# A hybrid decoder layer: S5 halves as two chains, recurrence gates two strips behind their input, ten gate strips ahead of the GLU, states through DRAM

## The chip, the core and the metric

The kernel runs on one core of a Trainium2 chip, in one launch. Its time is device microseconds (us) from launch to end, as the median of several executions; one more execution is taken with the hardware profiler, and all rows below come from that one. The core has a matmul engine (TensorE, PE in the rows; PEld are its weight loads), a vector engine (VectorE, DVE), an engine for activation functions (ScalarE, ACT), a general one (GpSimd, POOL), and SyncE (SP), whose queue issues every transfer between DRAM and on-chip memory (DMA).

## The reference

One decoder layer on 1024 tokens of width 1024, in fp32:

```
h  = rms_norm(x) ;  z = h @ w_in + b_in          # columns: u_a 512, u_b 1024, gate_a 1024, gate_b 1024
# S5 branch: 32 groups of 16 channels, 64 complex states each
s_t = A * s_{t-1} + B u_a ;  y = Re(C s) + d * u_a
z_a = gelu(y) ;  y_a = z_a * sigmoid(z_a @ w_glu + b_glu)
# RG-LRU branch
xc = causal conv of width 4 over u_b
r, i = sigmoid(xc @ w_r + b_r), sigmoid(xc @ w_i + b_i)      # 16 heads of 64
a = exp(-8 r softplus(-lambda)) ;  h_t = a h_{t-1} + sqrt(1 - a^2) i xc
merged = sigmoid(gate_a) * (y_a @ w_a_out) + sigmoid(gate_b) * (h @ w_b_out)
x = x + merged @ w_o
x = x + (silu(h2 @ w_gate) * (h2 @ w_up)) @ w_down           # h2 = rms_norm(x), hidden 2816
x = x + sigmoid(rms_norm(x) @ w_pg + b) * rms_norm(p @ w_ple)
out = rms_norm(x)
```

The change touches the S5 branch, the RG-LRU branch and the order of the matmuls between them; the feed-forward part and the end stay as they are.

## The kernel before, in words

Everything is held transposed: 128 channels on the partitions, 1024 tokens along the free axis; such a tile is a slot, and there are 43 slots (`NSLOT`, one pool, `slot`). A matmul in fp32 is done as three matmuls of a faster type: each operand is split into a high part (ACT copies it) and a low part (DVE subtracts), in `split` (L231, L232) for activations and in `prep_to` (L187, L188) for weights, and `mm3` (L220) adds high x high, high x low and low x high in PSUM. PSUM has four tiles of 128 x 1024; the same four serve the strips' sums (`mm`) and everything else (`sm`).

The work is a list of units (`add`, `plan`). A unit is one strip of 128 output channels: two chunks of four weight blocks, 48 matmuls in all (a GLU strip is one chunk of 24). `emit` traces a unit chunk by chunk: matmuls, then, behind the first chunk, the eviction of the unit before (`flush`), then the weights of later chunks, then one step (`tick`) of each running chain. A chain is a generator that does a piece of side work at each step; `drain` runs a chain to its end at once. Transfers, engine order and waits are then set by a planner that takes instructions in the traced order as they become ready; `tc.high_priority()` lets some go first. Engines work strictly in the order that the planner gives them.

Order of the units before: 8 units of `p @ w_ple`; 4 of u_a (`ev_ua` writes each to DRAM as `ud`); 9 gate strips (`add_gate`; gate_a 0 to 7 and gate_b 0, `ev_ga` and `ev_gb` scale them, take the sigmoid and write them to DRAM); 4 GLU strips; 1 gate strip; 8 of `w_a_out` (`add_ao`); then the 8 strips of u_b (`add_ub`, conv in `ev_ub` L576 and L579) with the small gate units of the recurrence (`add_ri`: 24 matmuls, r and i of 128 channels) one strip behind, and gate strips after strips 1, 2, 4 and 5, before the last gate unit and at the end; then 8 of `w_b_out`, 8 of `w_o`, and the rest.

S5 (`s5_all`) is one chain. `s5_params` prepares constants on POOL. `s5_setup(hf)`, six steps for each half of the groups: products of powers and B, C on DVE (L1319 to L1336), transposes (L1347), a convolution kernel for blocks of eight tokens (L1362 to L1369), which 16 transfers spread into `km`. `s5_data(hf)`: 16 transfers bring the half's input blocks from `ud` (`U`, L1413), `s5_tables` makes sine and cosine tables (ten DVE instructions, L1388 to L1398, and ACT's Abs and Sin), 64 matmuls project the input (L1432), twelve DVE instructions rotate it (L1440 to L1446), two scans and six more run the recurrence over blocks (L1448 to L1455), 96 matmuls make the output (`km` L1468, `wr`, `wi` L1473), and two copies (`Y`, L1480) and 32 transfers in all put it into `yd`. Both setups run one after the other, then the two halves' data steps take turns, one half at each step.

`pre_glu` drains S5 and then `load_z`, which for each of four tiles loads y from `yd`, takes gelu (`z`, L657) and splits it (`zh`, `zl`). The GLU's matmuls read these.

In the recurrence, `lru(m0)` takes strips in pairs, started by the eviction of the pair's second gate unit: exp, tanh, square (ACT, L610 to L616), products (DVE, L619, L621), sqrt (ACT, L623), product (L626), scan (DVE, L630). The eight states `yb` stay in slots until `yb_split` splits them for `w_b_out`; `pre_b` drains both.

Of the kernel before, what the change touches and what calls it, by code (L numbers as in the profile page):

```python
# [14 lines left out]
AF = mybir.ActivationFunctionType  # L15
ALU = mybir.AluOpType

P = 128
L = 1024
# [11 lines left out]
LOAD_AHEAD = 6  # L31
PREP_AHEAD = 4
DOWN_PARTS = (8, 7, 7)
GATES_FIRST = 9
UB_GATES = (1, 2, 4, 5)
X_POOL = ()
HEAD_UNITS = 10
TAIL_CUT = 768
# [56 lines left out]
class Build:  # L95
# [339 lines left out]
    def plan(self):  # L435
        nc, h = self.nc, self.h
# [5 lines left out]
        self.xd = self.dram([8, P, L], "xd")  # L442
        self.vd = self.dram([22, P, L], "vd")
        self.ud = self.dram([512, 8, P], "ud")
        self.yd = self.dram([512, 8, P], "yd")
        pt = {}

# [54 lines left out]
        for n2 in range(4):  # L502
            e = self.elem(lambda n2=n2: wple[n2 // 2][:, 512 * (n2 % 2):512 * (n2 % 2) + 512])
            for q in range(2):
                n = 2 * n2 + q
# [20 lines left out]
        def w_in(n):  # L526
            return self.chunks(h["w_in"][n], lambda k: xg[k])
# [33 lines left out]
        def add_gate():  # L561
            f, n, ev = gates.pop(0)
            self.add(f(n), ev)

        for m in range(GATES_FIRST):
            add_gate()


        xcs, xct, ri, yb = {}, {}, {}, {}

        def ev_ub(m):
            def ev(ps):
                u = scaled(ps, "x", "u")
                nc.scalar.activation(out=u, in_=u, func=AF.Identity, bias=self.v("b_in", 4 + m))
                xc = self.slot(name="xc")
                nc.vector.tensor_scalar(out=xc, in0=u, scalar1=self.v("conv_w", 24 + m), scalar2=self.v("conv_b", m),  # L576
                                        op0=ALU.mult, op1=ALU.add)
                for s in (1, 2, 3):
                    nc.vector.scalar_tensor_tensor(  # L579
                        out=xc[:, s:], in0=u[:, :L - s], scalar=self.v("conv_w", 8 * (3 - s) + m), in1=xc[:, s:],  # L580
                        op0=ALU.mult, op1=ALU.add)
                xct[m] = xc
                xcs[m] = self.split(xc, "xc")
            return ev

        def ri_mm(m):
            def mm(u, hi, lo, pairs):
                u.ps = [self.ps_sm(), self.ps_sm()]
                for q in range(2):
                    w = slice((2 * (m % 2) + q) * P, (2 * (m % 2) + q + 1) * P)  # L590
                    self.mm3(u.ps[q], hi[:, w], lo[:, w], xcs[m], True, True)
                xcs.pop(m)
            return mm

        def ev_ri(m):
            def ev(ps):
                for q, b in ((0, "b_r"), (1, "b_i")):
                    t = self.slot(name="ri")
                    nc.scalar.activation(out=t, in_=ps[q], func=AF.Sigmoid, bias=self.v(b, m))  # L599
                    ri[m, q] = t  # L600
                if m % 2 == 1:
                    self.lru_last = self.start(lru(m - 1))
            return ev

        def lru(m0):
            a, a2, th = {}, {}, {}
            ms = (m0, m0 + 1)
            for m in ms:
                a[m] = self.slot(name="a")
                nc.scalar.activation(out=a[m], in_=ri[m, 0], func=AF.Exp, scale=self.m8sp[:, m:m + 1])  # L610
            for m in ms:
                th[m] = ri.pop((m, 0))
                nc.scalar.activation(out=th[m], in_=th[m], func=AF.Tanh, scale=self.p8sp[:, m:m + 1])
            for m in ms:
                a2[m] = self.slot(name="a2")
                nc.scalar.activation(out=a2[m], in_=a[m], func=AF.Square)  # L616
            yield
            for m in ms:
                nc.vector.scalar_tensor_tensor(out=th[m], in0=a2.pop(m), scalar=1.0, in1=th[m],  # L619
                                               op0=ALU.add, op1=ALU.mult)  # L620
                nc.vector.tensor_tensor(out=ri[m, 1], in0=ri[m, 1], in1=xct.pop(m), op=ALU.mult)  # L621
            for m in ms:
                nc.scalar.activation(out=th[m], in_=th[m], func=AF.Sqrt)  # L623
            yield
            for m in ms:
                nc.vector.tensor_tensor(out=ri[m, 1], in0=ri[m, 1], in1=th.pop(m), op=ALU.mult)  # L626
            yield
            for m in ms:
                y = self.slot(name="yb")
                nc.vector.tensor_tensor_scan(out=y, data0=a.pop(m), data1=ri.pop((m, 1)), initial=0.0,  # L630
                                             op0=ALU.mult, op1=ALU.add)
                yb[m] = y
            yield

        ri_elem = {}
# [1 line left out]
        def add_ub(m):  # L637
            pre = None
            if m == 0:
                def pre():  # L640
                    self.lrup = self.start(self.lru_params())
            self.add(w_in(4 + m), ev_ub(m), pre=pre)

        def add_ri(m):
            if m // 2 not in ri_elem:
                ri_elem[m // 2] = self.elem(h["w_ri"][m // 2])
            self.add([(ri_elem[m // 2], None)], ev_ri(m), mm=ri_mm(m))


        ya, gl, mg, ybs = {}, {}, {}, {}  # L650

        def load_z():
            for m in range(4):
                y = self.slot(shape=(P, 8, P), name="y")
                nc.sync.dma_start(y, self.yd[m * P:(m + 1) * P])
                z = self.slot(name="z")
                nc.scalar.activation(out=z.rearrange("p (c j) -> p j c", j=8), in_=y, func=AF.Gelu_apprx_tanh)  # L657
                self.zs[m] = self.split(z, "z")
                self.zf[m] = z
                yield  # L660

        def load_g(kind, m):
            if m < 8 and (kind, m) not in gl:
# [1 line left out]
                nc.sync.dma_start(t, {"a": self.gad, "b": self.gbd, "p": self.apd}[kind][m])  # L665

        def pre_glu():
            self.drain(self.s5gen)
            self.drain(self.start(load_z()))

        def ev_glu(m):
            def ev(ps):
# [16 lines left out]
            return ev  # L689

        def yb_split():
            for m in range(8):
                while m not in yb:
                    yield
                ybs[m] = self.split(yb.pop(m), "yb")
                yield

        def pre_ao():
            load_g("a", 0)
# [4 lines left out]
        for m in range(4):  # L704
            add_glu(m)
            if m == 0:
                self.units[-1].pre = pre_glu
        add_gate()
        for m in range(8):
            add_ao(m)  # L710
        for m in range(8):
            add_ub(m)
            if m >= 1:
                add_ri(m - 1)
            if m in UB_GATES:
                add_gate()
        add_gate()
        add_ri(7)
        while gates:
            add_gate()  # L720
        self.units[-2].pre = lambda: setattr(self, "ybg", self.start(yb_split()))

        def pre_b():
# [393 lines left out]
    def s5_all(self):  # L1117
        self.zs, self.zf = {}, {}
        self.s5gen = self.chains[-1]
        yield from self.s5_params()  # L1120
        data = []
        for hf in range(2):
            yield from self.s5_setup(hf)
        while self.ua_done < 2:
            yield
        d0 = self.s5_data(0)
        d1 = self.s5_data(1)
        live = [d0]
        n = 0
        while live or n < 2:  # L1130
            if n < 2 and self.ua_done >= 4:
                n += 1
                if n == 2:
                    live.append(d1)
            for g in list(live):
                try:
                    next(g)
                except StopIteration:
                    live.remove(g)
                yield  # L1140

    def s5_params(self):
        nc, h = self.nc, self.h
# [261 lines left out]
    def s5_data(self, hf):  # L1405
        nc, st = self.nc, self.st

        us = []
        for i in range(2):
            u = self.slot(shape=(P, 8, P), name="U")  # L1410
            m = 2 * hf + i
# [25 lines left out]
        for q in range(2):  # L1437
            c = slice(512 * q, 512 * q + 512)
# [14 lines left out]
        nc.vector.tensor_tensor(out=co, in0=t2, in1=co, op=ALU.mult)  # L1453
        nc.vector.tensor_tensor(out=qr, in0=qr, in1=si, op=ALU.subtract)
        nc.vector.tensor_tensor(out=qi, in0=qi, in1=co, op=ALU.add)  # L1455
        yield
        wr, wi = st.pop(("w", hf))
        km = st.pop(("k", hf))
        psy = []
# [17 lines left out]
        for q in range(2):  # L1477
            m = 2 * hf + q
            y = self.slot(shape=(P, 8, P), name="Y")
            nc.scalar.activation(out=y.rearrange("p (a b) c -> p b a c", b=2),  # L1480
                                 in_=psy[q].rearrange("p (b a c) -> p b a c", b=2, a=4), func=AF.Copy)
# [70 lines left out]
```

## Time and profile before

| | us |
|---|---|
| median of 3 runs | 1487.66 (1486.79 to 1490.31) |
| profiled execution: time | 1488.67 |
| profiled execution: span, first to last instruction | 1486.7 |
| PE busy | 1423.7 (96% of the span) |
| DVE / ACT / POOL busy | 847.3 / 564.3 / 151.3 |
| TensorE's granted clock, mean | 0.976 of full speed |

PE's busy time counts matmuls at whatever clock is granted, so a stretch can be fully busy and still slow; the clock stands in a column of its own. In the rows, `out<-in` names tiles by their names in the program, with buffer numbers left out; a line number is that of the kernel, and can be that of a helper. Behind `<-` in square brackets stands what ended the idle time of the engine.

### The profile page before, as it was taken

The numbers are of one execution on the slowest core, as the hardware profiler recorded it, in microseconds if no ns is written. First come the engines' busy times: TensorE is split into PE (matmuls) and PEld (weight loads), VectorE is DVE, ScalarE is ACT, GpSimd is POOL, SyncE is SP. The second block draws the span as 40 slices with busy tenths as digits, with TensorE's granted clock in tenths as the row PEclk, the third lists the DMA queues.
The fourth block names the chain that finished last, engine by engine and source line by source line (L and its number), as shares of the span: only waits on it lengthen the run. The fifth ranks groups of instructions, "written<-read, shape, count | busy, mean of one in ns | idle before, by whom it ended". The sixth has DMA issues, their size and how long they took to land.

```text
span 1486.7 us, 16789 instructions
## 1 busy us (share of the span) xinstructions
PE 1423.7 (96%) x6586; PEld 1175.3 (79%) x6586; DVE 847.3 (57%) x988; ACT 564.3 (38%) x720; POOL 151.3 (10%) x250
## 2 busy tenths in 40 slices
PE   8899967999989899999999999999999999999995
PEld 6688856788878688887788888888888888888885
DVE  7366493535577774367566655555556224256486
ACT  7232132612554852144433333333335342123333
POOL 7910300000000000000000000000000021012243
PEclk9999987999999999999999999999999999999997
DMA  8322424351212144353122222222227442232222
GB/s 322 102 99 88 130 64 109 129 208 58 76 44 78 50 175 155 117 171 113 57 85 85 86 85 85 83 80 80 85 71 242 146 152 84 71 106 88 76 92 113
DMA packets 70318, 161.39 MB, mean 109 GB/s; under 512 B 11520, under 2 KB 23200, under 8 KB 70240
## 3 DMA queue, kind: packets, MB, share of 16 engines
q1 hardware_dynamic: 70240, 160.33, 32.0%
q8 instruction: 51, 0.84, 0.2%
q14 instruction: 27, 0.22, 0.0%
HBM read 118.23 MB, written 40.89 MB: 107 GB/s over the span
## 4 chain that ended last, share of the span: by engine, by line
PE 78%; DVE 7%; issue 5%; ACT 4%; POOL 4%; DMA 1%; SPq 1%; DVEq 0%; ACTq 0%; POOLq 0%
PE mm L220 47%; PE mm L312 28%; PE sm L220 1%; POOL x L963 1%; SPq L1483 1%; PE sm L392 0%; DVE x L1026 0%; DVE xc L579 0%; ACT ri L599 0%; DVE el L1016 0%; PE sm L1473 0%; ACT sq L410 0%; PE sm L377 0%; DMA s5p<-s5p 0%; DVE yb L630 0%
## 5 line engine op out<-in xcount | busy, mean ns | idle before, releaser
L187 ACT ACTIVATE whi<-raw 128x512 fp32r<-128x512 f32 (+1 forms) x158 | 97.3, 618 | 375.4 <-PE mm L220 322.9
L312 PE MATMUL mm<-twh,whi 128*128 128x512 f32 x528 | 206.5, 391 | 1.3 <-ACT pc L290 1.0
L312 PE MATMUL mm<-twl,whi 128*128 128x512 f32 x528 | 206.0, 390 | 0.8 <-DVE twl L232 0.8
L312 PE MATMUL mm<-twh,wlo 128*128 128x512 f32 x528 | 202.7, 390 | 0.0
L188 DVE TENSOR_TENSOR wlo<-raw,whi 128x512 fp32r<-128x512 f32 (+1 forms) x158 | 109.6, 696 | 128.8 <-ACT whi L187 128.8
L220 PE MATMUL mm<-xgh,whi 128*128 128x512 f32 x448 | 139.7, 393 | 0.0
L220 PE MATMUL mm<-xgh,wlo 128*128 128x512 f32 x448 | 138.0, 390 | 1.0 <-DVE wlo L188 1.0
L220 PE MATMUL mm<-xgl,whi 128*128 128x512 f32 x448 | 138.6, 390 | 0.0
L312 PEld LDWEIGHTS mm<-twh,whi 128*128 128x128 f32 x528 | 99.5, 188 | 23.1 <-ACT pc L290 1.4
L312 PEld LDWEIGHTS mm<-twl,whi 128*128 128x128 f32 x528 | 99.5, 189 | 22.0 <-DVE twl L232 1.1
L312 PEld LDWEIGHTS mm<-twh,wlo 128*128 128x128 f32 x528 | 99.4, 188 | 20.8
L174 ACT ACTIVATE whi<-wr 128x512 fp32r<-128x512 f32 x110 | 69.5, 632 | 105.7 <-PE mm L312 102.2
L220 PE MATMUL mm<-vh,wlo 128*128 128x512 f32 x352 | 109.0, 390 | 0.0
L220 PE MATMUL mm<-vl,whi 128*128 128x512 f32 x352 | 108.4, 389 | 0.0
L220 PE MATMUL mm<-vh,whi 128*128 128x512 f32 x352 | 108.3, 389 | 0.0
L412 POOL TENSOR_TENSOR acc<-acc,sq 128x1024 f32<-128x1024 f32 (+1 forms) x18 | 43.8, 2434 | 610.8 <-ACT sq L410 610.8
L220 PEld LDWEIGHTS mm<-xgh,whi 128*128 128x128 f32 x448 | 84.2, 189 | 18.7 <-issue 1.5
L220 PEld LDWEIGHTS mm<-xgh,wlo 128*128 128x128 f32 x448 | 83.9, 188 | 18.8 <-DVE wlo L188 1.4
L220 PEld LDWEIGHTS mm<-xgl,whi 128*128 128x128 f32 x448 | 84.2, 188 | 17.9 <-issue 0.3
L175 DVE TENSOR_TENSOR wlo<-wr,whi 128x512 fp32r<-128x512 f32 x110 | 74.6, 686 | 26.7 <-ACT whi L174 26.6
L220 PEld LDWEIGHTS mm<-vh,wlo 128*128 128x128 f32 x352 | 66.1, 188 | 14.0 <-issue 0.2
L220 PEld LDWEIGHTS mm<-vh,whi 128*128 128x128 f32 x352 | 66.1, 188 | 13.9 <-issue 0.2
(388 smaller groups left out, 2453.5 us busy)
## 6 DMA issues: line engine op xcount, KB each, us to landing
raw<-w_in SPq DMA_DIRECT2D x56, 256.0 KB, 2.7
wr<-w_gate SPq DMA_DIRECT2D x22, 512.0 KB, 5.2
wr<-w_up SPq DMA_DIRECT2D x22, 512.0 KB, 3.6
vd<-fv SPq DMA_DIRECT2D x22, 512.0 KB, 2.9
vr<-vd SPq DMA_DIRECT2D x22, 512.0 KB, 5.2
raw<-w_down SPq DMA_DIRECT2D x32, 256.0 KB, 2.7
el<-ed SPq DMA_DIRECT2D x16, 512.0 KB, 3.9
x<-xT SPq DMA_DIRECT2D x8, 512.0 KB, 7.8
```

The lines of the kernel that those rows point to most:

```text
L174: nc.scalar.activation(out=hi, in_=src, func=AF.Copy)
L175: nc.vector.tensor_tensor(out=lo, in0=src, in1=hi.bitcast(F32), op=ALU.subtract)
L187: nc.scalar.activation(out=hi[:, :w], in_=raw[:, :w], func=AF.Copy)
L188: nc.vector.tensor_tensor(out=lo[:, :w], in0=raw[:, :w], in1=hi[:, :w].bitcast(F32), op=ALU.subtract)
L220: nc.tensor.matmul(ps[:, t - t0:e - t0], w, v[:, t:e], start=(first and q == 0), stop=(last and q == 2),)
L312: nc.tensor.matmul(bank[b], w[:, k * P:(k + 1) * P], v, start=start and k == 0 and p == 0, stop=k == 3 and p == 2, skip_group_check=True)
L412: eng.tensor_tensor(out=a, in0=a, in1=s, op=ALU.add)
L963: (nc.gpsimd if eng else nc.vector).tensor_tensor(out=x, in0=x, in1=rstd["z"][:, :TAIL_CUT], op=ALU.mult)
L1483: nc.sync.dma_start(self.yd[m * P:(m + 1) * P, j, :].rearrange("(g p) c -> p g c", p=16), y[16 * j:16 * j + 16])
```

## The change

- `s5_all` starts two chains, one for each half (`s5_half`); the second waits three steps (`S5_STAGGER`) before it begins its setup. Each half goes on to its data steps by itself.
- In `s5_data`, four steps (`S5_LAG`) instead of one lie between the scans and the output matmuls.
- `load_z` is a chain of its own that waits for both halves; it issues all four loads in its first step, then takes gelu and splits in pairs.
- Ten gate strips stand ahead of the GLU (`GATES_FIRST`); behind the GLU stands the first u_b strip instead of a gate strip.
- The gate units of the recurrence follow their u_b strip by two strips (`RI_LAG`) instead of one; the gate strips between stand after strips 2, 3, 5 and 6, and one before the last gate unit.
- States 0 to 5 are written to DRAM (`ybd`) behind their scan, and `yb_split` loads them back, one ahead of the one that it splits.

```diff
-GATES_FIRST = 9
-UB_GATES = (1, 2, 4, 5)
+GATES_FIRST = 10
+UB_GATES = (2, 3, 5, 6)
+RI_LAG = 2
+S5_LAG = 4
+S5_STAGGER = 3
...
                                              op0=ALU.mult, op1=ALU.add)
-                yb[m] = y
+                if m < 6:
+                    nc.sync.dma_start(self.ybd[m], y)
+                yb[m] = y if m >= 6 else None
...
         def load_z():
+            while any(g in self.chains for g in self.s5c):
+                yield
+            y = {}
             for m in range(4):
-                y = self.slot(shape=(P, 8, P), name="y")
-                nc.sync.dma_start(y, self.yd[m * P:(m + 1) * P])
-                z = self.slot(name="z")
-                nc.scalar.activation(out=z.rearrange("p (c j) -> p j c", j=8), in_=y, func=AF.Gelu_apprx_tanh)
-                self.zs[m] = self.split(z, "z")
-                self.zf[m] = z
-                yield
+                y[m] = self.slot(shape=(P, 8, P), name="y")
+                nc.sync.dma_start(y[m], self.yd[m * P:(m + 1) * P])
+            yield
+            for m in range(4):
+                z = self.zf[m] = self.slot(name="z")
+                nc.scalar.activation(out=z.rearrange("p (c j) -> p j c", j=8), in_=y.pop(m), func=AF.Gelu_apprx_tanh)
+                if m % 2:
+                    yield
+                    for i in (m - 1, m):
+                        self.zs[i] = self.split(self.zf[i], "z")
...
         def pre_glu():
-            self.drain(self.s5gen)
-            self.drain(self.start(load_z()))
+            for g in (self.s5gen, *self.s5c, self.zgen):
+                self.drain(g)
...
         def yb_split():
+            t = {}
+
+            def load(m):
+                if m in yb:
+                    t[m] = yb.pop(m)
+                    if t[m] is None:
+                        t[m] = self.slot(name="yr")
+                        nc.sync.dma_start(t[m], self.ybd[m])
+
+            load(0)
             for m in range(8):
-                while m not in yb:
+                load(m + 1)
+                yield
+                while m not in t:
+                    load(m)
                     yield
-                ybs[m] = self.split(yb.pop(m), "yb")
-                yield
+                ybs[m] = self.split(t.pop(m), "yb")
...
-        add_gate()
+        add_ub(0)
         for m in range(8):
             add_ao(m)
         for m in range(8):
-            add_ub(m)
-            if m >= 1:
-                add_ri(m - 1)
+            if m:
+                add_ub(m)
+            if m >= RI_LAG:
+                add_ri(m - RI_LAG)
             if m in UB_GATES:
                 add_gate()
-        add_gate()
-        add_ri(7)
+        for m in range(8 - RI_LAG, 8):
+            if m == 7:
+                add_gate()
+            add_ri(m)
         while gates:
             add_gate()
...
         yield from self.s5_params()
-        data = []
-        for hf in range(2):
-            yield from self.s5_setup(hf)
-        while self.ua_done < 2:
+        self.zgen = self.start(self.load_z())
+        self.s5c = [self.start(self.s5_half(hf)) for hf in range(2)]
+
+    def s5_half(self, hf):
+        for _ in range(hf * S5_STAGGER):
             yield
-        d0 = self.s5_data(0)
-        d1 = self.s5_data(1)
-        live = [d0]
-        n = 0
-        while live or n < 2:
-            if n < 2 and self.ua_done >= 4:
-                n += 1
-                if n == 2:
-                    live.append(d1)
-            for g in list(live):
-                try:
-                    next(g)
-                except StopIteration:
-                    live.remove(g)
-                yield
+        yield from self.s5_setup(hf)
+        while self.ua_done < 2 * hf + 2:
+            yield
+        yield from self.s5_data(hf)
...
         nc.vector.tensor_tensor(out=qi, in0=qi, in1=co, op=ALU.add)
-        yield
+        for _ in range(S5_LAG):
+            yield
         wr, wi = st.pop(("w", hf))
```

## Rows read from the trace of the kernel before

**Rows 1.** The page, part 2: PE's busy tenths and granted clock in 40 slices.

```profile
PE   8899967999989899999999999999999999999995
...
PEclk9999987999999999999999999999999999999997
```

**Rows 2.** PE's waits to 640 us: engine, line, releaser, total, times, longest.

```profile
PE sm L1473 <- DVE q L1454: 12.4, 2, 12.0
PE mm L220 <- ACT zh L231: 10.3, 2, 6.8
PE sm L220 <- ACT xch L231: 6.3, 2, 3.5
...
PE sm L220 <- ACT ri L599: 2.9, 2, 1.7
```

**Rows 3.** Stretches: length, busy PE, PEld, DVE, ACT, POOL (instructions), clock, DMA, GB/s.

```profile
85.00:174.00 89.00, 89.00 (x499) 74.73 (x498) 48.11 (x51) 23.37 (x27) 13.79 (x51) 1.00 0.31 95
174.00:236.00 62.00, 49.58 (x331) 40.57 (x330) 60.71 (x63) 15.95 (x18) 0.76 (x2) 0.81 0.25 76
204.00:216.00 12.00, 1.17 (x6) 0.62 (x4) 12.00 (x11) 4.02 (x5) 0.00 (x0) 0.72 0.08 22
216.00:235.00 19.00, 17.85 (x96) 14.64 (x96) 19.00 (x19) 1.09 (x3) 0.00 (x0) 0.55 0.00 1
235.00:245.00 10.00, 9.55 (x93) 8.00 (x92) 0.41 (x1) 1.90 (x2) 0.00 (x0) 1.00 0.50 106
245.00:262.00 17.00, 6.94 (x19) 5.07 (x18) 1.23 (x1) 9.19 (x7) 0.00 (x0) 0.70 0.67 186
...
419.00:428.00 9.00, 4.96 (x11) 3.47 (x12) 6.60 (x7) 6.01 (x6) 0.00 (x0) 0.62 0.08 29
502.00:512.00 10.00, 4.90 (x12) 3.60 (x13) 9.44 (x7) 6.77 (x8) 0.00 (x0) 0.72 0.17 53
488.00:536.00 48.00, 42.85 (x177) 34.62 (x176) 37.51 (x32) 39.37 (x41) 0.00 (x0) 0.93 0.24 79
```

**Rows 4.** The chain that ended last, to 640 us: start, length, what.

```profile
254.71 4.25 DMA y<-yd
...
428.48 21.79 PE mm L220 x96
```

**Rows 5.** DVE's instructions in order of time, 80 to 245 us: start, length, what.

```profile
174.66 1.22 DVE L1388 TENSOR_TENSOR ph<-iota,gh 128x1024 f32<-128x1024 f32 x1
...
177.66 1.22 DVE L523 TENSOR_TENSOR ga<-mm,rb 128x1024 f32<-128x1024 f32 x1
...
234.19 1.22 DVE L1454 TENSOR_TENSOR q<-q,ph 128x1024 f32<-128x1024 f32 x1
```

**Rows 6.** The issues of SP's queue in order of time, 84 to 262 us.

```profile
158.84 10.30 SPq L1373 DMA_DIRECT2D km<-ks  x16
...
169.81 7.90 SPq L1413 DMA_DIRECT2D U<-ud  x16
...
246.09 8.52 SPq L1483 DMA_DIRECT2D yd<-Y  x16
```

**Rows 7.** ACT's instructions in order of time, 80 to 270 and 470 to 560.

```profile
248.74 2.03 ACT L657 ACTIVATE z<-y 128x1024 f32<-128x1024 f32 x1
250.80 1.06 ACT L231 ACTIVATE zh<-z 128x1024 fp32r<-128x1024 f32 x1
...
504.29 1.06 ACT L231 ACTIVATE xch<-xc 128x1024 fp32r<-128x1024 f32 x1 [2.13 <-DVE xc L579]
...
515.44 1.28 ACT L610 ACT_TABLE_LOAD   x1
516.73 2.19 ACT L610 ACTIVATE a<-ri,m8sp 128x1024 f32<-128x1024 f32 x2
```

**Rows 8.** The page, part 6: issues, count, KB each, us to landing.

```profile
vd<-fv SPq DMA_DIRECT2D x22, 512.0 KB, 2.9
vr<-vd SPq DMA_DIRECT2D x22, 512.0 KB, 5.2
```

More of the change, by code (lines that the diff above doesn't have):

```diff
@@ L444, in plan @@
         self.ud = self.dram([512, 8, P], "ud")
+        self.ybd = self.dram([8, P, L], "ybd")
         self.yd = self.dram([512, 8, P], "yd")
@@ L652, in load_z @@
         def load_z():
+            while any(g in self.chains for g in self.s5c):
+                yield
+            y = {}
             for m in range(4):
-                y = self.slot(shape=(P, 8, P), name="y")
-                nc.sync.dma_start(y, self.yd[m * P:(m + 1) * P])
-                z = self.slot(name="z")
-                nc.scalar.activation(out=z.rearrange("p (c j) -> p j c", j=8), in_=y, func=AF.Gelu_apprx_tanh)
-                self.zs[m] = self.split(z, "z")
-                self.zf[m] = z
-                yield
+                y[m] = self.slot(shape=(P, 8, P), name="y")
[8 more added lines that the diff above has]
+                        self.zs[i] = self.split(self.zf[i], "z")
+        self.load_z = load_z
         def load_g(kind, m):
```

## The prediction

> **What bounds the kernel now.** I read the slices of the page first: TensorE (PE) is busy eight or nine tenths nearly everywhere, with holes in slices 1, 5 to 7, 11, 13 and 19, and the granted clock dips in the same places [rows 1]. The program is a single stream of matmuls, so a gain can only come from PE idle time, or from PE time at the lower clock. Next I read PE's waits up to 640 us [rows 2]: 12.4 us for the last product of the S5 state (`q` L1454), 10.3 us for `zh`, the split input of the GLU, and 6.3 + 2.9 us before the recurrence's gate matmuls (`xch`, `ri`). The change touches these four rows and nothing else. Last, the stretches around them [rows 3] give the whole price, the clock included.
>
> S5 stretch. The ninth gate strip ends near 205.2 us (1.17 us of work after 204). Then:
> - 204 to 216: 12.00 - 1.17 = 10.8 us idle.
> - 216 to 235: half 0's output matmuls (96 of them) take 19.00 us at clock 0.55; half 1's same 96 take 9.55 us of 10.00 at clock 1.00. Lost: 19.00 - 9.55 = 9.5, and 0.5 more in 235 to 245.
> - 245 to 262: 19 matmuls, which at full clock take 19 x 0.227 = 4.3 us (21.79 us for 96 [rows 4]); 17.0 - 4.3 = 12.7 lost.
> Sum 33.5 us. VectorE (DVE) is the cause: busy 60.71 of 62 us from 174 to 236, and only 48.11 of 89 before [rows 3]. Its tables start at 174.66 and its last S5 product ends at 235.4 [rows 5].
>
> Recurrence. 419 to 428: 9.0 us for 11 matmuls (2.5 us), lost 6.5. 502 to 512: 10.0 us for 12 (2.7), lost 7.3, and some 0.5 at low clock behind it. Sum 14.3 us. Of these, 4.0 and 5.1 are idle and 2.5 to 2.7 each is clock: that is my price of the slow stretch behind one wait of 4 to 5 us.
>
> The ceiling is 33.5 + 14.3 = 47.8 us. The profiled execution took 1488.67 us (span 1486.7); the median is 1.0 less, and I give times on the median's scale: 1487.7 - 47.8 = 1439.9 at best.
>
> A rule on how to read this stands in the Trainium skill, "Perfetto Trace Analysis", Identifying the Most-Contended Engine: it says that matmul busy share misleads and that weight-load busy share is the better measure. From 216 to 235 matmul busy is 94% and weight-load busy 77% (84% in 85 to 174), so either share finds 1 to 2 us to win there, and only the clock column finds 9.5. By the rule the S5 sum would be some 8 us less, and the forecast 1460; by the rows the measurement decides, and I keep 33.5.
>
> **Part 1: the two chains.** Counting scheduler steps (one per weight chunk, 5.45 us of PE), half 0's tables move from step 29 to 24, its first products from 32 to 26, its scans from 36 to 28; half 1's scans move from 39 to 31, its output matmuls from 41 to 35, and these fall inside ten strips (steps 17 to 36) instead of behind nine. No instruction is added. What matters is whether DVE, whose work is unchanged, is done in time. From 85 on it has 48.1 + 60.7 us and 2.4 for the tenth strip: 111 us. On PE, nine strips end at 205 with setup and first products between them; half 0's output matmuls add 9.55, so half 1's are wanted at about 215. DVE has 130 us for 111 of work. It must wait for two things on the way: 16 `km` transfers take SP 10.3 us to issue, and 16 `U` transfers 7.9 [rows 6], and the tables stand behind the U tiles (the second tile's first issue falls at 173.8, `ph` starts at 174.66, and a gate strip's eviction stands behind it at 177.66 [rows 5]). Slots seem to be handed out in program order, and I take that to hold after too. With 12 us for such waits DVE ends near 208, 7 before it is wanted: no PE wait on `q`. Bounds: nothing, to all of DVE's 19 us of slack and more (rival C). For gate evictions behind U tiles I take 2 us of PE wait for a PSUM tile; below, nothing, as PE lost nothing in 85 to 174; above, the full issue time (rival E).
>
> **Part 2: what is late next, z.** `load_z` now starts when both chains are done, with all four `y` loads behind the last Y transfers. After half 1's output matmuls: copy of the second Y, 1.0; half of the 16 issues (8.52 us [rows 6]; the first Y's half runs under the matmuls), 4.3; load and landing of y, 4.25 [rows 4]; a table load 1.28; two gelus before the first split, 4.1; the split `zh`, 1.06 [rows 7]. Sum 16.0 us. Under it lies the tenth strip, 10.9. So PE waits 5.1 for z0, and pays 2.6 of slow clock behind it. Then z0 and z1 of three or four GLU units (8 to 11 us of matmuls) cover z2 and z3. Bounds: 0 if the first two loads are issued under half 1 (rival B), 16 + 2.6 if the strip is not behind the matmuls (rival C).
> Kept of S5: 33.5 - 2 - 5.1 - 2.6 = 23.8 us.
>
> **Part 3: one `u_b` strip instead of a gate strip behind the GLU.** Both are 48 matmuls, 10.9 us, and cover the last `ya` split alike. Its longer eviction (four `xc` passes) runs under the 87 us of `w_a_out`. Cost nothing; without that cover, some 4 us of DVE. It holds three slots for longer; the states that go to DRAM give back up to six.
>
> **Part 4: gates two strips behind.** A strip's chain is seven full-tile instructions (scale, bias, four `xc` passes, split) of about 1.2 us, some 8.5 in all. The last strip's split came at 504.29 [rows 7]; its strip had ended 13.6 (a gate unit and a gate strip) before 501.9, at 488.3. So the chain took 16, because the previous pair's exp/tanh/square stood between. Now gate 6 follows 27 us behind its strip, gate 7 behind two gate units and a strip (16.3 us instead of 13.6), and the pair's work is started after its strip's eviction instead of before it. I take both waits as gone, with 1 us left for two gate units in a row on four PSUM tiles (0 to 4.0, the older of the two idles). What is late next is the start of `w_b_out`: recurrence pairs 4,5 and 6,7 now both fall into the last two gate strips. From the end of the last `u_b` strip, ScalarE (ACT) did 39.37 us of work in 488 to 536 [rows 3]. Added: the sigmoids and exps that lay before 488 (4.0) and two table changes (2.6): 46 us. To do it in: 3 gate units and 2 strips, 8.2 + 21.8 = 30 us, and what `w_b_out` can start without the last states: before, it ran on without a wait for some 16 us until the last split was there. 46 against 46, and ACT had 8.6 us of waits of its own in these 48: a wait of 0 to 9, of which I take 2, since the evictions and splits before it are spread over three units.
> A rule on that term: the Trainium skill, "ScalarE: Activation LUTs", What ACT_TABLE_LOAD costs, has 2.66 us per change of set, a drain included. Here the load is 1.28 and the next ACTIVATE starts 0.01 after it [rows 7]; by the Trainium skill's figure the six changes there would cost 8 us more and the forecast would be rival D's 1460.
>
> **Part 5: states through DRAM.** Six writes and six reads of 512 KB. Nearest rows: 2.9 us to land a write, 5.2 a read [rows 8], and about 0.6 us of SP for each issue [rows 6]. States 0 to 3 have two strips or more. States 4 and 5 come out of their scans about when `w_b_out` starts and need 8.1 us; four k of three units (16 us of matmuls) come before them. Cost nothing; without the cover, 8.
> Kept of the recurrence: 14.3 - 1 - 2 = 11.3 us.
>
> **Sum.** 23.8 + 11.3 = 35.1; 1487.7 - 35.1 = 1452.6.
>
> **Rivals.**
> B, z is no wait: y0 and y1 are loaded while half 1 works, as before y0 was. For: half 0 is done three steps earlier. Against: slots in program order put them behind the last Y. 1452.6 - 7.7 = 1445.
> C, the chains do not do what they say: the planner, short of slots (both halves at once want some 40 of 43), leaves half 1's tables or scans late, and the output matmuls come after the tenth strip. Then the 16 us z chain lies bare (11 more), with a DVE delay up to 5: 1464 to 1469. For: DVE's slack is one part in seven. Against: 48.11 of 89 busy before 174 is room that nothing used.
> D, `w_b_out` waits 9 for ACT instead of 2: 1460. For: the budget above. Against: ACT waits less when its inputs come earlier.
> E, slower than before: gate evictions stand behind the U tiles, and those behind the km issues. If the tile not evicted is the one that PE wants next, PE waits 10.3 + 7.9 and 3.0 for the tables ahead of it, and 2.6 of clock: 23.8 per half, 47.6 instead of my 2: 1498. For: 177.66 behind 174.66. Against: four PSUM tiles, and an eviction held for 4 us cost PE nothing. It decides once these waits pass 37 us for both halves.
>
> **Numbers.** Forecast 0.43, B 0.16, C 0.19, D 0.11, E 0.07, and 0.04 that S5 or the recurrence wins nothing and the sum stays near the old time. The range reaches from 1438 (ceiling) to 1472 (C's end and some); E, the last 0.04 and part of C's tail are left out. The forecast's own range is 1447 to 1458. Faster by over 0.3% (4.5 us, what a measurement here can tell) 0.90, within 0.03, slower 0.07.
>
> **What would show it.** Right: no PE wait on `q` and both halves' output matmuls at clock 1.00, inside the strips; one wait of about 5 us on `zh`; the GLU running through from about 242 instead of 262; no `xch` wait before gate units. C shows as tables of half 1 later than 175 and a `zh` wait over 14. D shows as a wait on `ybh`. E shows as gate matmuls waiting for `ga` evictions around 140 to 190. I am wrong in the main if DVE's last S5 product ends after 215, or if a wait over 5 us appears between 265 and 560.

## The result, and the profile after

The changed kernel takes 1466.29 us (median of 4 runs, 1465.75 to 1467.20); the kernel before takes 1488.01 (4 runs). Ratio 0.9847, 95% interval 0.9829 to 0.9864: 21.7 us gained, where 35.1 were forecast. The profiled execution took 1465.75 us, its span 1463.8, 22.9 less than before. The measured median lies inside the stated range (1438 to 1472), but outside the forecast's own range of 1447 to 1458; the number fits rival C's. What follows shows that it is not rival C.

The first view is the page's slices, against [rows 1], counted from 1: slices 6 and 7 stood at six and seven tenths and are now at eight and nine. Slices 12 and 14 are at eight as before, and 13 and 19 have fallen to eight.

```profile
PE   8999989999988899998999999999999999999995
...
PEclk9999989999999999999999999999999999999997
```

PE's waits from 110 to 640 us, against [rows 2]:

```profile
PE mm L223 <- ACT ri L603: 4.4, 1, 4.4
PE sm L223 <- ACT ri L603: 3.9, 1, 3.9
PE sm L1488 <- DVE q L1462: 3.7, 1, 3.7
PE mm L223 <- ACT ybh L234: 2.3, 1, 2.3
PE mm L223 <- ACT whi L190: 1.7, 1, 1.7
PE mm L223 <- ACT zh L234: 1.6, 1, 1.6
PE mm L223 <- DVE ybl L235: 0.4, 1, 0.4
```

The wait on `q` fell from 12.4 to 3.7, that on `zh` from 10.3 to 1.6, and `xch` no longer appears. But `ri` (the evictions of the gate units) grew from 2.9 to 8.3, and 4.4 us stand at the start of `w_b_out`, where PE waited for nothing before.

The stretches, with the columns of [rows 3]. First S5, then the two gate waits, then the start of `w_b_out`:

```profile
85.00:154.00 69.00, 69.00 (x457) 58.52 (x456) 50.33 (x53) 21.80 (x25) 5.32 (x19) 1.00 0.33 102
154.00:186.00 32.00, 32.00 (x187) 26.77 (x187) 31.86 (x36) 6.30 (x8) 22.67 (x33) 1.00 0.43 124
186.00:194.00 8.00, 4.32 (x20) 3.24 (x19) 4.01 (x7) 6.24 (x6) 0.00 (x0) 0.91 0.12 33
194.00:208.00 14.00, 13.98 (x97) 11.59 (x97) 14.00 (x14) 2.30 (x3) 0.00 (x0) 0.68 0.27 94
208.00:219.00 11.00, 11.00 (x50) 9.10 (x50) 5.27 (x6) 2.83 (x4) 0.00 (x0) 1.00 0.50 106
219.00:229.00 10.00, 10.00 (x101) 8.88 (x100) 1.82 (x2) 2.27 (x3) 0.00 (x0) 1.00 0.56 201
...
402.00:412.00 10.00, 6.08 (x21) 4.49 (x20) 7.80 (x9) 6.53 (x7) 0.00 (x0) 0.83 0.16 54
461.00:471.00 10.00, 5.56 (x19) 4.19 (x18) 5.46 (x5) 6.85 (x7) 0.00 (x0) 0.83 0.08 28
492.00:506.00 14.00, 9.98 (x37) 7.48 (x36) 10.96 (x10) 11.05 (x12) 0.00 (x0) 0.88 0.59 203
```

Half 1's 96 output matmuls run at clock 1.00 and take 9.1 us (219.2 to 228.3). Half 0's 96 come behind the 3.7 us wait and take 14.0 us (194.0 to 208.0) at 0.68: some 4.9 us of clock behind 3.7 of wait. The forecast had 2 us for a PSUM wait, and no clock.

When each stage of PE's stream begins, from the first matmul of each stage in the traces (us):

| | before | after | moved |
|---|---|---|---|
| GLU | 251.9 | 240.8 | -11.1 |
| `w_a_out` | 291.0 | 273.6, behind a `u_b` strip of 10.9 that stood later before | -17.4 |
| end of `w_a_out` | 334.7 | 317.2 | -17.4 |
| end of `w_a_out` to `w_b_out` | 188.9 | 174.9, without that strip | -14.0 |
| `w_b_out` itself | 87.0 | 93.7 | +6.7 |
| `w_o` | 610.6 | 585.9 | -24.7 |
| end of span | 1486.7 | 1463.8 | -22.9 |

The `u_b` strip 0 now stands between GLU and `w_a_out`. With it taken out on the side after, the time up to `w_a_out` fell by 291.0 - (273.6 - 10.9) = 28.3, of which 2.8 fell before 107 us, where nothing was changed (this head is short in seven of the experiments' profiled executions and some 2 us longer in the other five, though no edit touches it). So S5 gave 25.5. From the end of `w_a_out` to `w_b_out`: 188.9 - (174.9 + 10.9) = 3.1 gained; `w_b_out` lost 6.7. The recurrence therefore lost 3.6 where 11.3 were forecast, and the FFN and the tail lost 1.8. Sum 2.8 + 25.5 - 3.6 - 1.8 = 22.9. The last 1.8 is not the change's either, as far as the traces show: the FFN up to its down projection is the same code everywhere and takes 430.2 us before and in e3, 431.8 in the changed kernel and most others, and 433.4 in e1, e9 and e12.

### The profile page after: what moved, and what is told of

Same layout as the page of the kernel before. It is cut to its first block, busy times and chain, and to the rows that moved or that the text cites. A ratio compares the mean times of both kernels' runs of the same rounds, so it can differ in the third digit from the quotient of the medians.

```text
span 1463.8 us, 16823 instructions
## 1 busy us (share of the span) xinstructions
PE 1415.7 (97%) x6586; PEld 1171.3 (80%) x6586; DVE 848.9 (58%) x988; ACT 565.6 (39%) x722; POOL 164.4 (11%) x250
## 4 chain that ended last, share of the span: by engine, by line
PE 78%; issue 5%; DVE 5%; ACT 5%; POOL 4%; SPq 1%; DMA 1%; DVEq 0%; POOLq 0%; ACTq 0%
PE mm L223 46%; PE mm L315 28%; PE sm L1488 1%; PE sm L1493 1%; PE sm L223 1%; POOL x L992 1%; SPq L1392 1%; ACT ri L603 1%; POOL el L1054 0%; DVE yb L634 0%; DVE x L1055 0%; PE sm L380 0%; DVE xc L583 0%; SPq L1432 0%; DVE el L1045 0%
```

## The experiments

Each group of experiments has its own runs of the kernel before, to which the ratios refer: 1489.67 us for e1 to e4, 1489.39 for e5 to e8, 1489.28 for e9 to e11, 1490.40 for e12. "e7" stands for e7_gates_357, and so on.

**e1_lag1: the gate units one strip behind, as before.**

```
-RI_LAG = 2               +RI_LAG = 1
-UB_GATES = (2, 3, 5, 6)  +UB_GATES = (1, 2, 4, 5)
```

> The changed kernel with its gate units of the recurrence one strip behind their input again, and the gate strips between them back after strips 1, 2, 4 and 5. All else as changed (two S5 chains, ten strips ahead, states through DRAM). Theory: two strips behind only turned the wait for the split xch into a wait of the same length for a PSUM tile, because ACT evicts a gate unit (ri) behind that same split; from the end of w_a_out to the end of w_b_out the changed kernel loses 18.5 us (11.8 to the start of w_b_out, 6.7 in it), the kernel before lost 14.9, and pairs 4,5 and 6,7 lie further apart with one strip. So 1460 to 1464 us, about 4 faster than the changed kernel's 1466.3, with xch waits of 6 us back and no wait in w_b_out. Rival (the lag does what it says, and the waits left have another cause): the xch waits come on top, 1470 to 1478.

Measured 1468.58 us (ratio 0.9861, interval 0.9847 to 0.9874); both missed. The `xch` wait of 6.3 is back and `w_b_out` takes 90.5, but from the end of `w_a_out` to `w_o` it is 268.4 us, against 268.6 in the changed kernel. The lag of two strips gains at one place what it loses at the others. The 2.3 us between the medians do not lie in this stretch: of the 3.9 us between the profiled runs, 3.0 lie behind the start of `w_o`, where the edit touches nothing.

**e2_states_in_slots: states stay on the chip.**

```
-                if m < 6:
-                    nc.sync.dma_start(self.ybd[m], y)
-                yb[m] = y if m >= 6 else None
+                yb[m] = y
```

> The changed kernel with states 0 to 5 kept in their slots, no write to DRAM and no load back. Theory: the loads of states 4 and 5 stood on SP behind a weight load that waited for its buffer until 501.6 us, ACT sat 4.5 us for them, and w_b_out lost 6.7 us in all; without them w_b_out loses 2 to 3, so 1461 to 1464 us. Rival (43 slots do not hold the states beside strips that live two strips longer): splits wait for slots, 1467 or more. Second rival (ACT's and DVE's own work sets the end of the last states): within 1 us of 1466.3.

Measured 1466.38 (0.9848): no difference, and `w_b_out` again takes 93.7. The way through DRAM neither cost nor hid anything; the forecast's "cost nothing" stands.

**e3_gate_evict_first: a gate unit's two evictions are written right behind its matmuls, ahead of the strip's that came before.**

```
             if ci == 0:
+                if u.mm is not None:
+                    u.ev(u.ps)
                 self.flush()
...
-        self.pend = lambda: u.ev(u.ps)
+        if u.mm is None:
+            self.pend = lambda: u.ev(u.ps)
```

> The changed kernel with the eviction of a gate unit (two sigmoids, ri) traced before the eviction of the strip ahead of it, instead of a unit later. Theory (ACT's order: the sigmoids stand behind xch, and PE finds no PSUM tile): the waits of 3.9 us near 403 and 4.4 us near 462 go, with some 3 us of slow clock behind them, 1455 to 1460 us if the start of w_b_out stays as it is. Rival (DVE is late with the strip's conv behind the two scans, and whatever reads it waits): the wait turns up again at xch or at w_b_out, 1464 to 1468.

Measured 1465.45 (0.9841, interval 0.9826 to 0.9856): by the medians no different from the changed kernel, as the rival had it. Both `ri` waits of the changed kernel are gone; a new one stands at gate unit 7, and the wait for `ybh` at the start of `w_b_out` has grown from 2.3 to 5.0:

```profile
PE mm L223 <- ACT ybh L234: 5.0, 1, 5.0
PE sm L223 <- ACT ri L606: 4.4, 1, 4.4
```

So ScalarE's (ACT) order decides which unit waits. Gate unit 6's sigmoids (478.56) stand behind the exp, tanh and square of the pair before (471.09 to 477.25), as they do in the changed kernel; with the wait ahead of it gone, PE comes to gate unit 7 earlier and finds no second free tile. In this profiled run the stretch to `w_o` is 265.5 us instead of 268.6; the long slow stretch in S5 shown in the last section hides that.

**e4_one_chain: S5 as one chain as before, LAG 1; everything else as changed.**

```
-        self.zgen = self.start(self.load_z())
-        self.s5c = [self.start(self.s5_half(hf)) for hf in range(2)]
+        for hf in range(2):
+            yield from self.s5_setup(hf)
...
-S5_LAG = 4   +S5_LAG = 1
```

What is left out is the kernel before's own code: both `s5_data` in turns in the one chain, and `load_z` drained at the GLU.

> The changed kernel with S5 as one chain again: both setups, then the halves' data steps in turn, one step between scans and output matmuls. The ten strips, the first strip of u_b behind the GLU, the new z loads and the whole recurrence stay. Theory (the two chains carry most of the S5 gain of 25.5 us, because DVE's tables and scans start earlier; a tenth strip by itself covers at most its 10.9 us): 1478 to 1484 us, with PE waiting again for half 0's last S5 product. Rival (the tenth strip is the gain, the chains only move work that was hidden): 1465 to 1470.

Measured 1484.22 (0.9963, interval 0.9949 to 0.9977), at the upper end of the theory. The `zh` waits are 9.2 and the `q` waits 5.7 again: the chains, with their lag of four steps and z's own chain, carry some 18 of the 21.7 us. The three were not taken apart.

**e5_psv_copied: half 1's first products leave PSUM at once.** It goes for the wait on `q` in the changed kernel. PE's instructions there, in order of time (start, length, what, idle before and its releaser):

```profile
173.85 0.60 PE L1451 MATMUL sm<-U,vbi 128*64 128x128 f32 x4
...
194.02 1.19 PE L1488 MATMUL sm<-U,km 128*128 128x128 f32 x4 [3.70 <-DVE q L1462]
```

DVE's, of the same kernel, in the same view:

```profile
168.94 1.21 DVE L1407 TENSOR_TENSOR ph<-iota,gh 128x1024 f32<-128x1024 f32 x1
...
178.72 1.22 DVE L1473 TENSOR_TENSOR q<-q,ph 128x1024 f32<-128x1024 f32 x1
...
191.39 0.69 DVE L1459 TENSOR_TENSOR q<-sm,pw 128x512 f32<-128x512 f32 x1 [3.99 <-ACT pw L1421]
...
193.20 0.68 DVE L1462 TENSOR_TENSOR q<-sm,ph 128x512 f32<-128x512 f32 x1
...
196.19 2.34 DVE L527 TENSOR_TENSOR ga<-mm,rb 128x1024 f32<-128x1024 f32 x2
...
211.36 1.21 DVE L1473 TENSOR_TENSOR q<-q,ph 128x1024 f32<-128x1024 f32 x1
```

Half 0's last product ended at 179.9, ten us before its output matmuls were wanted. They waited for room in PSUM, whose four tiles serve strips and S5 alike. Half 1's first products lay in two of them from 174. The other two held the sums of two gate strips, done at 179.4 and 190.3, whose evictions (`ga`) stood on VectorE (DVE) behind those products, at 196.19. DVE read the first of the products' tiles only from 191.39 to 193.88: half 1's tables, mixed with half 0's last products on a full DVE (31.86 of 32 us in 154 to 186), were done by 186.8 and ACT's sines behind them at 191.4. To put the two gate evictions ahead of the products on DVE would have been another cure; it was not run. The releaser is named `q`, as in the wait before, but it frees a tile and delivers no input.

```
+            if hf:
+                c = slice(512 * q, 512 * q + 512)
+                nc.scalar.activation(out=t2[:, c], in_=ps[:, 0:512], func=AF.Copy)
+                nc.scalar.activation(out=t1[:, c], in_=ps[:, 512:1024], func=AF.Copy)
...
```

Half 1's four `q` products then read `t1` and `t2`. The text below speaks of a small pool of two tiles; the program has one pool of four, for strips and S5 alike.

> The second half's two first products are copied out of PSUM by ScalarE as soon as they are there (four copies of 128x512), and VectorE forms the q products from the copies; nothing else is edited. Theory: in the changed kernel TensorE stands 3.7 us at 190.3 because both PSUM tiles of the small pool hold those products until VectorE has read them behind the second half's tables, and the clock stays at 0.5 behind it, another 4.7 us. With the copies the tiles are free some 14 us earlier: the wait and the slow stretch are gone (8.4 us), of which VectorE's last product (212.6, not earlier than before) and the z wait take back 2 to 4 us: 1459 to 1463 us. Rival 1: the second half's chain on VectorE sets when the GLU can begin (last product 212.6, output 9, z some 12.5 us behind), so the 8.4 us come back whole as a wait for z: 1465 to 1467. Rival 2: the wait had another cause (VectorE's products of the first half, or a late output request), then a wait at 190 stays: 1465 to 1467 with the wait in its old place.

Measured 1468.50 (0.9850, interval 0.9829 to 0.9872). PE's waits from 110 to 640 us:

```profile
PE mm L223 <- ACT zh L234: 6.3, 1, 6.3
...
PE sm L1505 <- DVE q L1485: 1.1, 1, 1.1
```

The wait and its clock loss are gone (half 0's output matmuls, with three of a gate strip among them, take 9.8 us at clock 1.00). All of it comes back at the GLU, which starts at 240.46 instead of 240.78: rival 1, though the median lies 1.5 above its range (the ratio is that of the changed kernel, 0.9847, within its interval). That half 1's products held the tiles is confirmed as the cause of the 3.7 us, and taking the wait away is worth nothing while the second half's way to z stays as it is.

**e6_gate_to_end: two gate strips instead of one behind the last gate unit.**

```
-UB_GATES = (2, 3, 5, 6)  +UB_GATES = (2, 4, 6)
```

> UB_GATES = (2, 4, 6) in place of (2, 3, 5, 6): one gate strip less between the u_b strips, two instead of one behind the last gate unit. Theory: w_b_out loses 6.7 us in the changed kernel because the last two states, split from memory and scanned late, have one strip (10.9 us) of cover; with two strips the waits at its start (2.3, 1.7) and its slow clock go: w_b_out back to 87 us and 1459 to 1462 us. Rival: the strip taken out from between the u_b strips covered ScalarE's and VectorE's own work there, and the waits for the gate units' evictions grow by as much (3 to 7 us more at L603): 1465 to 1469 with w_b_out at 87.

Measured 1462.03 (0.9819, interval 0.9801 to 0.9837). `w_b_out` takes 91.0; from the end of `w_a_out` to `w_o` 262.6 instead of 268.6, though one strip waits 5.6 for `ri`. Nearer to the theory: cover before `w_b_out` is worth part of the loss, and it is not taken back before it.

**e7_gates_357: e3's edit, and gate strips where two gate units stood back to back.**

```
-UB_GATES = (2, 3, 5, 6)  +UB_GATES = (3, 5, 7)     (with e3's edit)
```

> UB_GATES = (3, 5, 7) and a gate unit's eviction is written ahead of the u_b strip's: no two gate units stand back to back any more, and two strips follow the last one. Theory: the recurrence loses by two causes, ScalarE's sigmoids standing in its queue behind an xch that waits for the conv (3.9 and 4.4 us at the gate units), and too little cover at w_b_out (6.7 us). Each edit takes one away: 1455 to 1460 us. Rival: ScalarE's and VectorE's work in this stretch ends when it ends, the waits move to other units and to the start of w_b_out: 1463 to 1467, with the time from the end of w_a_out to w_o between 264 and 268 us (268.6 in the changed kernel).

Measured 1456.09 (0.9772, interval 0.9756 to 0.9789), inside the theory's range. PE's waits from the end of S5 to 640 us:

```profile
PE mm L223 <- ACT ybh L234: 2.7, 1, 2.7
PE mm L223 <- DVE ybl L235: 2.3, 1, 2.3
```

Between `w_a_out` and `w_b_out` there is no wait any more: 163.0 us, no more than its 13 strips of 10.9 and eight gate units of 2.7 (a gate unit is 12 matmuls in the traces, not 24). Together with `w_b_out` it is 258.0, 10.6 under the changed kernel: that much of the recurrence's forecast is there once the order allows it. The theory's second half failed: `w_b_out` takes 95.0, more than the 93.7 it was to mend, in spite of the longer cover. The gate strips' places without e3's edit were not run, so the two edits' shares are open.

**e8_all: e5 and e7 together.** The diff is the sum of the two.

> The copies of the second half's first products and the two edits of the gate order together. Theory: the stages are separate, so the gains add: 1450 to 1457 us. Rival: what S5 gains is given back as a wait for z, or what the gates gain is given back at w_b_out, and the sum is no better than the better one of the two alone: 1458 to 1466.

Measured 1455.44 (0.9771). The number lies in the theory's range, but the gains do not add: e7 alone has 1456.09, and what e5 gains is given back before the GLU here too (`zh` 6.3). The mechanism is the rival's.

**e9_states_in_slots2 and e10_split_earlier: is `w_b_out` late by its loads, or by when the splits are asked for?** On top of e7, e2's edit, and for e10:

```
-        self.units[-2].pre = lambda: setattr(self, "ybg", ...)
+        self.units[-3].pre = lambda: setattr(self, "ybg", ...)
```

> The gate order of e7, and the first six states kept on the chip instead of going through DRAM. In e7 the start of w_b_out waits 5.0 us for splits of states (ACT idle 4.8 us for their loads). Theory: here, unlike in e2, the loads are what is late, so w_b_out goes from 95 to 88 to 91 us: 1449 to 1453 us. Rival: the splits are late by the work of ScalarE and VectorE ahead of them, as e2 had it: within 1.5 us of e7.

> The gate order of e7, and the loads and splits of the states asked for one strip (10.9 us) earlier. Theory: the first splits stand behind a Sqrt, a strip's loads and a table load in ScalarE's queue only because they are asked for late; w_b_out 88 to 91 us: 1449 to 1453 us. Rival: they move ahead of the last states' own Sqrt and scans, which then come later: w_b_out stays at 94 to 96 us or waits in its sixth to eighth chunk, within 1.5 us of e7.

Measured 1457.78 (0.9793) and 1455.62 (0.9767), with `w_b_out` at 95.4 and 95.2: both rivals, e9's 0.2 us beyond its 1.5. The stretch at the start of `w_b_out` in e7 says why:

```profile
481.00:491.00 10.00, 4.98 (x17) 3.48 (x16) 10.00 (x9) 6.89 (x8) 0.00 (x0) 0.83 0.53 188
491.00:576.00 85.00, 85.00 (x369) 70.24 (x369) 42.28 (x43) 22.37 (x28) 0.00 (x0) 0.98 0.49 170
```

DVE is busy for all of the ten us, among other things with the last two scans, and PE's second wait there names DVE's `ybl`. ACT's wait for the loads, on which e9's theory rested, was beside the path.

**e11_z_by_halves and e12_z_behind_Y: the way to z, on top of e8.** e11 loads, makes and splits z of half 0 as soon as half 0's output is written:

```
-            while any(g in self.chains for g in self.s5c):
-                yield
+            y = {}
+            for hf in range(2):
+                while self.s5c[hf] in self.chains:
+                    yield
...
```

Behind it stand the loads, gelus and splits of this half's two z.

> The kernel e8 (copied first products, gate order of e7), and z of the first half loaded, made and split when the first half's output is written, not when both are. Theory: the first GLU chunk then waits for the second half's z alone, and later in its own course: the wait of 6.3 falls to 2 to 4 us, and e8's 8 us at the PSUM wait become worth something: 1449 to 1453 us. Rival: the second half's z (its load lands some 11 us behind the Y eviction) sets the same start, and the wait only moves by the 2.7 us that two K blocks take: 1453 to 1456 us.

Measured 1455.78 (0.9779, interval 0.9756 to 0.9803; 1452.85 to 1460.31): no difference from e8, in the rival's range. The profiled run begins the GLU at 232.04 and then waits 5.84 inside it. ACT's order shows why:

```profile
222.03 1.28 ACT L672 ACT_TABLE_LOAD   x1 [5.41 <-DMA y<-yd]
223.32 4.16 ACT L672 ACTIVATE z<-y 128x1024 f32<-128x1024 f32 x2
227.26 1.98 ACT L1515 ACTIVATE Y<-sm 128x1024 f32<-128x1024 f32 x2
...
239.84 2.05 ACT L672 ACTIVATE z<-y 128x1024 f32<-128x1024 f32 x1 [7.42 <-DMA y<-yd]
```

Half 1's output had been in PSUM from 222.4, but its copy stood behind a z that waited for its load, and the whole chain to the last z with it. e12 writes the first z behind that copy (`yw` holds the halves whose copies are written):

```
+            while 0 not in self.yw:
+                yield
+            load((0, 1))
+            yield
+            while 1 not in self.yw:
+                yield
+            gelu((0, 1))
+            load((2, 3))
...
```

> As e11, but the first half's z stands behind the second half's output evictions in ScalarE's queue (in e11 these evictions stood 4.9 us behind a z that waited 5.4 us for its load). Theory: the second half's output is written 3 to 4.9 us earlier, so its z too; GLU begins at about 232 as in e11 and the wait in its first strip falls from 5.8 to 1 to 3 us: 3 to 5 us under e11's profiled 1451.8, a median of 1449 to 1452 us. Rival: a strip's weights stand ahead of the first z in ScalarE's queue and wait for TensorE (4.9 us in e5), so the GLU begins at 236 or later and the gain goes: 1453 to 1456 us.

Measured 1450.21 (0.9733, interval 0.9710 to 0.9756; 1447.40 to 1452.87), as the theory had it and the lowest median of all (its interval only touches those of e7, e8 and e11, and is well clear of the changed kernel's). ACT's instructions in the same place:

```profile
222.25 1.94 ACT L1528 ACTIVATE Y<-sm 128x1024 f32<-128x1024 f32 x2 [5.84 <-PE sm L1521]
224.21 1.28 ACT L672 ACT_TABLE_LOAD   x1
225.50 4.12 ACT L672 ACTIVATE z<-y 128x1024 f32<-128x1024 f32 x2
...
235.05 2.21 ACT L672 ACTIVATE z<-y 128x1024 f32<-128x1024 f32 x1 [0.90 <-DMA y<-yd]
```

And PE's waits in S5:

```profile
PE mm L223 <- ACT zh L234: 1.3, 1, 1.3
PE sm L1521 <- DVE q L1501: 1.1, 1, 1.1
```

The GLU begins at 233.25 and `w_a_out` at 266.06, 7.5 earlier than in the changed kernel. In S5 all that is left of PE's waits is 2.4 us.

## Why the prediction was right or wrong

**S5, Parts 1 and 2: right in sum (25.5 measured, 23.8 forecast), wrong in its parts.** That DVE is done in time held: its last product ended at 212.6 where 208 was forecast, and half 1's matmuls ran at 219 without a wait. e4 shows that the two chains make the gain. What was taken as 2 us for PSUM in the setup (none there: 85 to 186 is full) came later, at half 0's output matmuls, as 3.7 us plus some 4.9 of clock: by then all four tiles were held, two of them by half 1's products, which the working did not count. So two of the signs of being right failed, no wait on `q` and clock 1.00 for both halves. And z cost 1.6, not 7.7. The working charged z's chain one long sequence from the last Y; the trace has the first two y loads issued under half 1, at 222.03, as rival B had it, and the first z at 235.27, behind a weight split that stood 3.2 us for PE, and not behind its load. The two errors nearly cancel, so that the sum fits is luck; some 2 us of the 25.5 are not accounted for (33.5 - 3.7 - 4.9 - 1.6 = 23.3).

**Recurrence, Part 4: this step failed.** "I take both waits as gone, with 1 us left for two gate units in a row", and 2 us at `w_b_out`. The `xch` waits are gone as said, but the three places in the windows above cost 10.0 - 21 x 0.227 = 5.2 us, 10.0 - 19 x 0.227 = 5.7 and 6.7: 17.6, where 3 were forecast and 14.3 stood before. The working asked when a gate's input is ready, and not behind what its eviction stands. ACT at the first of the three places:

```profile
396.83 1.15 ACT L578 ACTIVATE u<-u,vec 128x1024 f32<-128x1024 f32 x1 [7.14 <-DVE u L527]
397.88 0.61 ACT L190 ACTIVATE whi<-raw 128x512 fp32r<-128x512 f32 x1
403.30 1.06 ACT L234 ACTIVATE xch<-xc 128x1024 fp32r<-128x1024 f32 x1 [4.80 <-DVE xc L583]
404.37 1.28 ACT L603 ACT_TABLE_LOAD   x1
405.66 2.12 ACT L603 ACTIVATE ri<-sm,vec 128x1024 f32<-128x1024 f32 x2
```

The sigmoids of gate unit 2, whose matmuls were done at 390.7, stand in ACT's queue behind the `xch` of the strip that came just before it. ACT stands idle there for DVE's `xc`, which stands behind a pair's scans. At the second place (462) no scan is in the way: two gate units in a row fill all four PSUM tiles, and the sigmoids of the first stand behind the `xch` of a strip that had ended only at 456.35. The data wait of PE (9.2 us in all before) has turned into a wait for PSUM (8.3). e1 (sum 268.4 against 268.6), e3 (the waits move when the order does) and e7 (both `ri` waits go when the evictions come first and no two gate units stand in a row, 10.6 us) show this. What makes `w_b_out` longer stays open in part: no run brought it back to 87.0 (90.0 in e3, behind the wait of 5.0; 90.5 in e1, 91.0 in e6, 95.0 in e7), and e2 and e9 show that it is not the loads. Of the missing 13.4 us, 14.9 are this term; S5 and the head gave 4.5 more than forecast, the FFN and the tail took 1.8, and the medians differ by 1.2 less than the spans.

**Part 3 and Part 5: right.** The `u_b` strip behind the GLU covered the `ya` split without a wait; e2 and e9 put the way through DRAM at nothing.

**The rivals.** B's mechanism (the first y loads under half 1) happened, but earned 6 us, and the PSUM wait took more than that. C's time came true and C did not: half 1's tables began at 168.94, and the `zh` wait was 1.6. D named the right place, with 6.7 instead of 9. Its cause was to be ACT; in the changed kernel the waits there are 2.3 and 1.7 for ACT and 0.4 for DVE, and in e7's order DVE is full there. E's long waits did not come, but its mechanism did in small: gate evictions that stood on DVE behind half 1's work are two of the four tiles missing at 190. A time alone would have picked the wrong rival. (The prediction's list of slices with holes names 7 and 19 too, which have nine tenths by its count from 0; no sum rests on it.)

## What to carry to other kernels

When a step is moved to take away a wait for its input, follow its output too: on an engine that works in order, the eviction of a finished PSUM tile stands behind whatever waits there, and the wait comes back as one for a free tile. A releaser in the list of waits may deliver data or free a buffer; which of the two it is decides the cure. And a wait taken off ahead of a chain that ends later is worth nothing until that chain is shortened (e5: some 8 us gone, none gained; with e12's order behind it, 5 to 6).

## What the runs showed of the hardware

The price of one and the same wait was not constant. Behind the 3.7 us wait of S5 the granted clock was 0.50, the lower of its two levels (1.2 GHz of 2.4), from 194.0 to 202.9 in the changed kernel and 1.00 from there to 208; PE was busy throughout. Six other kernels with that wait (e1, e2, e6, e7, e9, e10) take about as long for half 0's output. In e3, whose wait is as long and whose work behind it is the same, the clock stayed at the lower level for some ten us longer, from 196.4 to about 215:

```profile
192.00:200.00 8.00, 4.29 (x22) 3.19 (x20) 6.19 (x10) 3.73 (x5) 0.00 (x0) 0.71 0.00 1
200.00:210.00 10.00, 10.00 (x54) 8.21 (x54) 10.00 (x8) 2.13 (x2) 0.00 (x0) 0.50 0.37 131
210.00:220.00 10.00, 10.00 (x51) 8.32 (x51) 4.99 (x5) 1.94 (x2) 0.00 (x0) 0.71 0.16 33
```

The same holds at the start of the FFN: with the same waits, e11 has clock 0.90 in its first 35 us (from 660.9; 119 matmuls in 30.2 us of busy PE) and e12 0.85 (from 655.2; 112 in 30.2), and the FFN up to the down projection is 431.8 us in the one and 433.4 in the other. With several waits of this kind per execution, such steps of 2 to 5 us may explain part of the spread between runs of one kernel, which is not shown; with the long slow stretch above, e3's profiled run came out 2.6 us over its median. Why the clock recovers sooner or later was not settled.
